# MLP in eight stages of d_ff, with w_down as a 2x2x2 Strassen scheme whose weight sums run on GpSimd

## The chip, the cores and the metric

The kernel runs on one core of one Trainium2 chip. The metric is device time in microseconds (us), from the first to the last instruction of the program with what the runtime lays around it; lower is better. A core has a matrix engine (PE, TensorE), three engines for element-wise work (DVE or VectorE, ACT or ScalarE, POOL or GpSimd) and a sync engine (SP) that issues the DMAs here. SBUF is the on-chip memory, PSUM the memory into which PE writes its products.

## The reference

One layer of a hybrid decoder on 256 tokens of width 2048, in float32. The change touches only the MLP behind the mixers (D_FF is 8192):

```python
    for l in range(DEPTH):
        x = x + hybrid_mixer(x, ln_mix_g[l], w_in[l], ...)
        hm = rmsnorm(x, ln_mlp_g[l]) @ w_up[l]
        x = x + jnp.square(jax.nn.relu(hm)) @ w_down[l]
    return rmsnorm(x, final_g)
```

`w_up` is 2048 x 8192, `w_down` 8192 x 2048. Each is 64 MB and is read once.

## The kernel before

**Precision.** Every float32 operand of a large product is split into two parts that PE takes in its faster float32 format: `hi` is the rounded value, `lo` what is left. A product of two split operands is made of three matmuls (hi hi, hi lo, lo hi). ACT writes `hi` (a cast), DVE then writes `lo = raw - hi`.

**Weight stream.** The weights arrive in pieces of 1 MB (128 partitions x 2048), in the order of use, through one queue of SP. A piece is split in two units of 128 x 1024 (`split_unit`, L131 for `hi` on ACT, L132 for `lo` on DVE). `advance(h)` is called ahead of each unit's matmuls; it issues loads up to 12 units and splits up to 4 units ahead. The buffers are 4 for `raw` and 5 each for `hi` and `lo`.

**The MLP.** d_ff is worked through in four quarters. In a quarter, 16 pieces of `w_up` come first: `mm_t` (L218, L219) multiplies a 128 x 128 tile of w_up with all 256 tokens; the moving operand holds both parts of the tokens side by side, so a `hi` weight runs 512 columns and a `lo` weight 256. DVE and ACT then add the halves, square what is above zero and split the result into `u` (L672 to L677). After this come 16 pieces of `w_down`, in four chunks of 512 output columns: `mm_n` (L237 to L239) takes, for each of 16 tiles of d_ff and each of the two token halves, three matmuls of 512 columns. A chunk is 96 matmuls and ends with an update of the residual `xr` on DVE (L691, PSUM and SBUF in). The last chunk is followed by the final norm and the output's DMAs.

**Order.** POOL runs in program order; on the other engines a scheduler places the instructions by priority and readiness, and the splits have a raised priority. Apart from the mixers and the final norm (L697, `xr` times the norm's gain) POOL has no work.

Of the kernel before, what the change touches and what calls it, by code (L numbers as in the profile page):

```python
# [14 lines left out]
P = 128  # L15
# [8 lines left out]
DFF = 8192  # L24
NQ = 4
# [4 lines left out]
DMA_AHEAD = 12  # L30
# [11 lines left out]
# columns of the packed per-partition vectors  # L42
# [10 lines left out]
# pieces of the packed rows  # L53
# [5 lines left out]
def trunk(ctx: ExitStack, tc: tile.TileContext, x, xt, w_t, w_n, w_o, w_u, w_d, gw, gm_w, cols, rows, out):  # L59
    nc = tc.nc  # L60
    const = ctx.enter_context(tc.tile_pool(name="const", bufs=1))
    big = ctx.enter_context(tc.tile_pool(name="big", bufs=1))
    wpool = ctx.enter_context(tc.tile_pool(name="wpool", bufs=W_BUFS))
    work = ctx.enter_context(tc.tile_pool(name="work", bufs=1))
    two = ctx.enter_context(tc.tile_pool(name="two", bufs=2))
    small = ctx.enter_context(tc.tile_pool(name="small", bufs=1))
    acc = ctx.enter_context(tc.tile_pool(name="acc", bufs=2, space=PSUM))
    misc = ctx.enter_context(tc.tile_pool(name="misc", bufs=4, space=PSUM))
# [18 lines left out]
    def load_piece():
# [3 lines left out]
        if j == 0:  # L91
            for i in range(4):
                if i < 2:
                    ks = slice(0, 1) if i == 0 else slice(1, 4)
                    nc.sync.dma_start(xs4[:, ks, :], xt3[:, ks, :])
                nc.sync.dma_start(raw[:, i * 512:(i + 1) * 512], pieces[j][:, i * 512:(i + 1) * 512])
        elif j < 4:
            for i in range(2):
                k = 4 * j + 2 * i
                nc.sync.dma_start(xs4[:, k:k + 2, :], xt3[:, k:k + 2, :])  # L100
                nc.sync.dma_start(raw[:, i * 1024:(i + 1) * 1024], pieces[j][:, i * 1024:(i + 1) * 1024])
        else:
            nc.sync.dma_start(raw, pieces[j])
# [10 lines left out]

    def split_unit():
        """w = hi + lo exactly, both in float32r's significand."""
        h = state["split"]
        state["split"] += 1
        parts = 1
        if h < 4 * UNITS:  # L120
            kn = 4 // UNITS
            for k in range(h * kn, (h + 1) * kn):
                x_prep(k)
            parts = 2 if h < P2 else 1
        raw = raws[h // UNITS][:, h % UNITS * UW:(h % UNITS + 1) * UW]
        hi = wpool.tile([P, UW], F32R, tag="hi", name=f"hi{h}")
        lo = wpool.tile([P, UW], F32R, tag="lo", name=f"lo{h}")
        n = UW // parts
        for i in range(parts):
            s = slice(i * n, (i + 1) * n)  # L130
            nc.scalar.copy(hi[:, s], raw[:, s])  # L131
            nc.vector.tensor_tensor(out=lo[:, s], in0=raw[:, s], in1=hi[:, s].bitcast(F32), op=ALU.subtract)  # L132
        his[h], los[h] = hi, lo
        if h % UNITS == UNITS - 1:
            raws.pop(h // UNITS)

    def advance(h):
# [36 lines left out]
    # constants that the mixers use  # L174
    cmask = const.tile([P, P], F32, name="cmask")
# [18 lines left out]
    def diag_broadcast(dst, col2, name):  # L194
        """dst[p, t] = col2[t % P, t // P] on every partition p."""
# [28 lines left out]
    def mm_n(pt, act, j, tail=0):  # L224
# [3 lines left out]
        n = 4 * UNITS  # L228
# [17 lines left out]
        if tail:  # L246
            advance(j * UNITS + n - 1)
# [14 lines left out]
    mm_n(pt, xg, 0)  # L262
# [524 lines left out]
```

## Time and profile before

| | |
|---|---|
| median of 3 runs | 1108.7 us (1108.28 to 1109.09) |
| span of the profiled execution | 1106.8 us; its whole time is not listed apart, the median of the runs is 1.9 us more than this span |
| PE busy | 1096.3 us, 99% |
| DVE busy | 693.6 us, 63% |
| ACT busy | 529.0 us, 48% |
| POOL busy | 56.6 us, 5% |
| granted PE clock | 0.998 of full speed |
| DMA | 211 MB, 190 GB/s of HBM over the span |

Busy time of PE is the sum of pipelined instructions, so its share only says that PE nearly always had something in flight. How long a stage takes is better read from the start times of its instructions, or from the windows of the stages. The times of DVE and POOL instructions in a timeline are from issue to completion: an instruction that is held up after its issue shows a longer duration, not idle time ahead of it.

### The profile page before, as it was taken

Reading aid. Unit: us, or ns where it says so; the run is one execution under the profiler, and the core shown is the slowest. Engines: PE = TensorE matmul, PEld = TensorE weight load, DVE = VectorE, ACT = ScalarE, POOL = GpSimd, SP = SyncE. Lnnn points to the kernel's source line nnn. Section 1 sums busy time; section 2 is a strip of 40 time slices with the busy share of each in tenths; the row PEclk is TensorE's granted clock in tenths of the full one; section 3 lists DMA queues with packets and bytes.
Section 4 is the critical chain, followed back from the end, with each engine's and each line's share of the span. In section 5 each row is a group of like instructions: output and inputs, shape, how many; then the busy total and the mean of one; then the engine's idle time right before and its main releaser. Section 6 shows DMA issues by size and latency. Waiting matters only on the chain.

```text
span 1106.8 us, 13675 instructions
## 1 busy us (share of the span) xinstructions
PE 1096.3 (99%) x5447; PEld 924.4 (84%) x5447; DVE 693.6 (63%) x841; ACT 529.0 (48%) x655; POOL 56.6 (5%) x70
## 2 busy tenths in 40 slices
PE   9999999999999999999999999999999999999997
PEld 7888888888888888888888888888888888888885
DVE  6799999565765566555456565455565545565553
ACT  7575754545554454443344443334444334444442
POOL 1002110040300000000000000000000000000111
PEclk9999999999999999999999999999999999999999
DMA  9645545455475555555555555555555555555541
GB/s 341 265 171 190 170 173 190 159 184 191 158 299 189 190 191 184 183 186 198 199 191 183 181 181 198 198 197 183 181 182 192 198 197 192 179 184 187 194 144 76
DMA packets 32175, 211.05 MB, mean 191 GB/s; under 512 B 3696, under 2 KB 4080, under 8 KB 7664
## 3 DMA queue, kind: packets, MB, share of 16 engines
q1 hardware_dynamic: 32112, 210.19, 53.9%
q8 instruction: 42, 0.69, 0.2%
q14 instruction: 21, 0.17, 0.0%
HBM read 208.08 MB, written 2.10 MB: 190 GB/s over the span
## 4 chain that ended last, share of the span: by engine, by line
PE 95%; issue 2%; DMA 1%; ACT 1%; POOL 1%; SPq 0%; DVE 0%; ACTq 0%; POOLq 0%
PE up L218 20%; PE up L219 10%; PE dn L239 10%; PE dn L237 10%; PE dn L238 10%; PE qk L218 5%; PE wo L237 3%; PE wo L239 3%; PE wo L238 3%; PE qk L219 3%; PE up L222 1%; PE o L237 1%; PE o L239 1%; PE o L238 1%; PE v L237 1%
## 5 line engine op out<-in xcount | busy, mean ns | idle before, releaser
L132 DVE TENSOR_TENSOR lo<-raw,hi 128x1024 fp32r<-128x1024 f32 (+1 forms) x388 | 477.7, 1233 | 365.8 <-ACT hi L131 364.9
L131 ACT CAST hi<-raw 128x1024 fp32r<-128x1024 f32 (+1 forms) x388 | 403.2, 1042 | 516.1 <-PE dn L239 188.7
L218 PE MATMUL up<-x,hi 128*128 128x512 f32 x960 | 341.9, 399 | 0.0
L219 PE MATMUL up<-x,lo 128*128 128x256 f32 x960 | 269.7, 281 | 0.0
L218 PEld LDWEIGHTS up<-x,hi 128*128 128x128 f32 x960 | 180.4, 188 | 41.6
L237 PE MATMUL dn<-hi,u 128*128 128x512 f32 x480 | 186.7, 389 | 0.0
L238 PE MATMUL dn<-lo,u 128*128 128x512 f32 x480 | 186.7, 389 | 0.0
L239 PE MATMUL dn<-hi,u 128*128 128x512 f32 x480 | 186.7, 389 | 0.0
L219 PEld LDWEIGHTS up<-x,lo 128*128 128x128 f32 x960 | 181.3, 189 | 3.1
L238 PEld LDWEIGHTS dn<-lo,u 128*128 128x128 f32 x480 | 90.1, 188 | 18.9
L239 PEld LDWEIGHTS dn<-hi,u 128*128 128x128 f32 x480 | 90.1, 188 | 18.8
L237 PEld LDWEIGHTS dn<-hi,u 128*128 128x128 f32 x480 | 90.1, 188 | 18.3
L218 PE MATMUL qk<-xg,hi 128*128 128x512 f32 x240 | 85.8, 400 | 0.0
L219 PE MATMUL qk<-xg,lo 128*128 128x256 f32 x240 | 67.4, 281 | 0.0
L310 DVE SCALAR_TENSOR_TENSOR cvo<-aT,colv,cvo 128x256 f32<-128x256 f32 x120 | 55.1, 511 | 0.0
L218 PEld LDWEIGHTS qk<-xg,hi 128*128 128x128 f32 x240 | 45.1, 188 | 10.5
L237 PE MATMUL wo<-hi,mix 128*128 128x512 f32 x128 | 50.4, 394 | 0.0
L238 PE MATMUL wo<-lo,mix 128*128 128x512 f32 x128 | 50.1, 391 | 0.0
L239 PE MATMUL wo<-hi,mix 128*128 128x512 f32 x128 | 49.9, 390 | 0.0
L697 POOL TENSOR_TENSOR xr<-xr,fgv 128x512 f32<-128x512 f32 x6 | 9.5, 1606 | 771.3 <-ACT jf L695 771.3
L219 PEld LDWEIGHTS qk<-xg,lo 128*128 128x128 f32 x240 | 45.3, 189 | 0.7
L239 PEld LDWEIGHTS wo<-hi,mix 128*128 128x128 f32 x128 | 24.0, 188 | 5.0
(232 smaller groups left out, 1076.0 us busy)
## 6 DMA issues: line engine op xcount, KB each, us to landing
raw<-in_w_u SPq DMA_DIRECT2D x64, 1024.0 KB, 4.7
raw<-in_w_d SPq DMA_DIRECT2D x64, 1024.0 KB, 4.7
raw<-in_w_n SPq DMA_DIRECT2D x28, 1024.0 KB, 4.7
raw<-in_w_t SPq DMA_DIRECT2D x16, 1024.0 KB, 4.8
raw<-in_w_o SPq DMA_DIRECT2D x16, 1024.0 KB, 4.8
raw<-in_w_n SPq DMA_DIRECT2D x6, 512.0 KB, 8.3
xr<-in_x SPq DMA_DIRECT2D x2, 1024.0 KB, 6.4
out<-xr SPq DMA_DIRECT2D x8, 256.0 KB, 2.6
```

The source lines that it names most:

```text
L131: nc.scalar.copy(hi[:, s], raw[:, s])
L132: nc.vector.tensor_tensor(out=lo[:, s], in0=raw[:, s], in1=hi[:, s].bitcast(F32), op=ALU.subtract)
L218: nc.tensor.matmul(pt[:, i, :], start=(k == 0), stop=False, **a)
L219: nc.tensor.matmul(pt[:, i, 0:T], start=False, stop=False, **b)
L222: nc.tensor.matmul(pt[:, i, :], start=False, stop=True, **a)
L237: nc.tensor.matmul(pt[t], lhsT=xh, rhs=hi[:, kk, :], start=(k == 0), stop=False)
L238: nc.tensor.matmul(pt[t], lhsT=xh, rhs=lo[:, kk, :], start=False, stop=False)
L239: nc.tensor.matmul(pt[t], lhsT=xl, rhs=hi[:, kk, :], start=False, stop=(k == NK - 1))
L310: nc.vector.scalar_tensor_tensor(out=o, in0=a, scalar=w, in1=o, op0=ALU.mult, op1=ALU.add)
L697: nc.gpsimd.tensor_tensor(out=xr[:, t, cs], in0=xr[:, t, cs], in1=fgv[:, cs], op=ALU.mult)
```

## The change

**Stages.** d_ff is cut into eight stages of 1024. Stage 0's eight w_up pieces run alone. Then, for each of seven stages, eight slots follow: a slot is one piece of w_down of this stage (`dn_piece`) and one piece of w_up of the next (`up_tile`). In the last stage there are four w_down slots alone, and its second half of the output columns is done the old way (`mm_n`, two chunks of 48 matmuls).

**Strassen.** A w_down slot covers two tiles of d_ff (256 rows) and 1024 output columns, that is, four weight blocks of 128 x 512, and the two token halves. The 8 block products become 7, so 21 matmuls instead of 24. PE's 1536 matmuls of 512 columns for w_down become 60 x 21 + 96 = 1356. The matmuls of w_up stay 64 tiles of 32.

**Weight sums.** For each of the 60 w_down slots POOL forms four sums of blocks in three instructions (`sum_piece`): one of 128 x 1024 (two sums that share a block, into `sa`), and two of 128 x 512 (into `sb`). There are two buffers for these, one for `sa` and one for `sb`. ACT and DVE then split 1536 + 1024 + 1024 columns per w_down piece (three blocks of `raw`, then `sa`, `sb`) where it was 2048.

**Activations.** After a w_up tile ACT copies one half, DVE adds the halves (L769, PSUM and SBUF in), takes the part above zero times the norm's factor `rb` (L770, both inputs in SBUF), and ACT squares it into `uf` (L771). For each pair of tiles POOL forms four sums in three instructions (L773, L775, L776), and ACT and DVE split seven blocks of 128 (`split_pair`, L791).

**Results.** Every four slots `dn_out` works the seven products into `xr`: a copy on ACT, seven additions on DVE (each with one input in PSUM, one in SBUF) and four of 128 x 512 on POOL (all in SBUF).

The core of the diff:

```diff
+    for st in range(NS - 1):
+        for sl in range(2 * NP):
+            jdn[st, sl] = len(pieces)
+            pieces.append((w_pair(st, sl), True))
+            jup[st + 1, sl] = len(pieces)
+            pieces.append((w_u[(st + 1) * 2 * NP + sl], False))
...
+    def sum_piece():
+
+        j = state["sum"]
+        state["sum"] += 1
+        if not pieces[j][1]:
+            return
+        raw = raws[j]
+        s13 = ph["mlp"].tile([P, 1024], F32, tag="sum", name=f"sa{j}", bufs=2)
+        s24 = ph["mlp"].tile([P, 1024], F32, tag="sum", name=f"sb{j}", bufs=2)
+        nc.gpsimd.tensor_tensor(out=s13.rearrange("p (a n) -> p a n", a=2),
+                                in0=raw[:, 512:1536].rearrange("p (a n) -> p a n", a=2),
+                                in1=raw[:, 0:512].rearrange("p (a n) -> p a n", a=1).broadcast_to([P, 2, 512]),
+                                op=ALU.add)
+        nc.gpsimd.tensor_tensor(out=s24[:, 0:512], in0=s13[:, 512:1024], in1=raw[:, 512:1024], op=ALU.add)
+        nc.gpsimd.tensor_tensor(out=s24[:, 512:1024], in0=s24[:, 0:512], in1=raw[:, 1536:2048], op=ALU.add)
+        sums[j] = (s13, s24)
...
+        if not pieces[j][1]:
+            src, n, tag, pool, bufs = raws[j][:, k * UW:(k + 1) * UW], UW, "", wpool, None
+        elif k == 0:
+            src, n, tag, pool, bufs = raws[j][:, 512:2048], 1536, "3", ph["mlp"], 2
+        else:
+            src, n, tag, pool, bufs = sums[j][k - 1], 1024, "", wpool, None
...
+        while state["sum"] < len(pieces) and state["sum"] <= j + SUM_AHEAD:
+            with tc.high_priority(HP):
+                sum_piece()
...
+        nc.vector.tensor_tensor(out=q, in0=pt[:, 0:T], in1=sb, op=ALU.add)
+        nc.vector.scalar_tensor_tensor(out=q, in0=q, scalar=0.0, in1=rb, op0=ALU.max, op1=ALU.mult)
+        nc.scalar.activation(u[:, 0:8:7, :] if i == 0 else u[:, 1:3, :], q.rearrange("p (t n) -> p t n", t=2), AF.Square)
+        if i == 1:
+            nc.gpsimd.tensor_tensor(out=u[:, S3:S1 + 1, :], in0=u[:, A21:A21 + 1, :].broadcast_to([P, 2, P]),
+                                    in1=u[:, A11:A22 + 1:2, :], op=ALU.subtract)
+            nc.gpsimd.tensor_tensor(out=u[:, S2, :], in0=u[:, A11, :], in1=u[:, S1, :], op=ALU.subtract)
+            nc.gpsimd.tensor_tensor(out=u[:, S4, :], in0=u[:, A12, :], in1=u[:, S2, :], op=ALU.subtract)
...
+        for k, prods in enumerate((((A11, 1), (S4, 0), (A12, 2)), ((S1, 1), (S3, 0)), ((S2, 0), (A22, 1)))):
+            advance(h0 + k)
+            hi, lo = his.pop(h0 + k), los.pop(h0 + k)
+            for a, b in prods:
...
+                nc.tensor.matmul(acc7[a], lhsT=ah, rhs=hi[:, cs], start=(g == 0), stop=False)
+                nc.tensor.matmul(acc7[a], lhsT=ah, rhs=lo[:, cs], start=False, stop=False)
+                nc.tensor.matmul(acc7[a], lhsT=al, rhs=hi[:, cs], start=False, stop=(g == NP - 1))
...
+        p1, v, w = (mlp.tile([P, 512], F32, tag=n, name=f"{n}{st}_{pn}") for n in ("p1", "v", "w"))
+        nc.scalar.copy(p1, acc7[A11])
+        dve(x12, x12, acc7[S4], ALU.add)
+        dve(x11, x11, acc7[A12], ALU.add)
+        dve(x12, x12, acc7[S1], ALU.add)
+        dve(x22, x22, acc7[S1], ALU.add)
+        dve(v, p1, acc7[S2], ALU.subtract)
+        dve(w, v, acc7[S3], ALU.subtract)
+        dve(x21, x21, acc7[A22], ALU.add)
+        pool(x11, x11, p1, ALU.add)
+        pool(x12, x12, v, ALU.subtract)
+        pool(x21, x21, w, ALU.add)
+        pool(x22, x22, w, ALU.subtract)
...
+    for st in range(NS - 1):
+        for sl in range(2 * NP):
+            pn, g = divmod(sl, NP)
+            if g == 0:
+                acc7 = {}
+            dn_piece(st, sl, acc7)
+            if pn == 1 and g < NP - 1:
+                split_pair(st + 1, g)
+            if g == NP - 1:
+                dn_out(st, pn, acc7)
+            up_tile(st + 1, sl)
+        split_pair(st + 1, NP - 1)
```

**POOL's order.** This is POOL's queue of the kernel before from the end of the mixers to the program's end (`lnc` and `og` belong to the mixers):

```order
L192 TENSOR_TENSOR lnc<-lnr,nhalf 128x2
L605 TENSOR_TENSOR og<-og,numx 128x512 x2
L697 TENSOR_TENSOR xr<-xr,fgv 128x512 x6
L192 TENSOR_TENSOR rf<-rf,nhalf 128x1 x2
```

The change puts 336 instructions of the MLP ahead of the last two of these lines: 180 for sums of weights, 96 for sums of activations, 60 for `xr`. This is POOL's queue of the change for two slots of the first mixed stage and the end of its first four slots:

```order
L159 TENSOR_TENSOR sa_3943<-raw_3749 128x1024
L163 TENSOR_TENSOR sb_3944<-sa_3943,raw_3749 128x512
L164 TENSOR_TENSOR sb_3944<-sb_3944,raw_3749 128x512
L159 TENSOR_TENSOR sa_4034<-raw_3847 128x1024
L163 TENSOR_TENSOR sb_4035<-sa_4034,raw_3847 128x512
L164 TENSOR_TENSOR sb_4035<-sb_4035,raw_3847 128x512
L823 TENSOR_TENSOR xr<-xr,p_0_4072 128x512
L823 TENSOR_TENSOR xr<-xr,v_0_4073 128x512
L823 TENSOR_TENSOR xr<-xr,w_0_4074 128x512 x2
L773 TENSOR_TENSOR uf_1_4024<-uf_1_4024 128x256
L775 TENSOR_TENSOR uf_1_4024<-uf_1_4024 128x128
L776 TENSOR_TENSOR uf_1_4024<-uf_1_4024 128x128
```

What moved: weight sums, the updates of `xr` and the sums of activations stand in one queue, each behind the one ahead of it.

**DVE's order.** This is DVE's queue of the kernel before for one pair of w_up tiles (all `raw` are w_up pieces):

```order
L132 TENSOR_TENSOR lo_4777<-raw_4590,hi_4776 128x1024
L674 TENSOR_TENSOR u_t_4768<-up_4681,u_sb_4766 128x512
L675 SCALAR_TENSOR_TENSOR u_t_4768<-u_t_4768 128x512
L132 TENSOR_TENSOR lo_4797<-raw_4590,hi_4796 128x1024
L677 TENSOR_TENSOR u_4588<-u_t_4768,u_4588 128x2x256
L132 TENSOR_TENSOR lo_4819<-raw_4632,hi_4818 128x1024
L132 TENSOR_TENSOR lo_4839<-raw_4632,hi_4838 128x1024
```

And this is DVE's queue of the change for one slot of the first mixed stage (`raw_4031` is the w_down piece of the slot after next, `raw_3982` a w_up piece):

```order
L769 TENSOR_TENSOR uq_3_4132<-up_3_4087,usb_3_4130 128x256
L770 SCALAR_TENSOR_TENSOR uq_3_4132<-uq_3_4132,rb 128x256
L190 TENSOR_TENSOR lo_4262<-raw_4031,hi_4261 128x1536
L791 TENSOR_TENSOR us_0_4187<-uf_0_3840,us_0_4187 128x7x128
L190 TENSOR_TENSOR lo_4176<-sa_4142,hi_4175 128x1024
L190 TENSOR_TENSOR lo_4194<-sb_4143,hi_4193 128x1024
L190 TENSOR_TENSOR lo_4214<-raw_3982,hi_4213 128x1024
L190 TENSOR_TENSOR lo_4249<-raw_3982,hi_4248 128x1024
L190 TENSOR_TENSOR lo_4272<-sa_4243,hi_4271 128x1024
```

What moved: the splits of w_down's sums (`sa`, `sb`) stand between those of `raw`, and wait on POOL's sums and ACT's casts of them; the splits of w_up stand behind them in the same queue.

## Rows read from the trace of the kernel before

**Rows 1.** The page, parts 1 and 4: busy time by engine, and the chain

```profile
PE 1096.3 (99%) x5447; PEld 924.4 (84%) x5447; DVE 693.6 (63%) x841; ACT 529.0 (48%) x655; POOL 56.6 (5%) x70
...
PE 95%; issue 2%; DMA 1%; ACT 1%; POOL 1%; SPq 0%; DVE 0%; ACTq 0%; POOLq 0%
```

**Rows 2.** Waits in total, DVE's largest (us, times, longest)

```profile
DVE lo L132 <- ACT hi L131: 364.9, 285, 2.4
```

**Rows 3.** Windows: head, one w_up and one w_down stage, last stage (columns as header)

```profile
core 0: us, PE busy (x) PEld busy (x) DVE busy (x) ACT busy (x) POOL busy (x), PEclk, DMA share, GB/s
0.00:387.60 387.60, 385.29 (x1856) 321.55 (x1857) 293.89 (x442) 220.69 (x311) 46.00 (x62) 1.00 0.57 205
...
566.20:656.90 90.70, 90.70 (x515) 78.66 (x514) 53.76 (x55) 40.96 (x47) 0.00 (x0) 1.00 0.54 186
656.90:743.90 87.00, 87.00 (x386) 72.09 (x385) 45.28 (x42) 34.74 (x35) 0.00 (x0) 1.00 0.56 194
```

**Rows 4.** Timeline, DVE from 71 us (start, duration, instruction)

```profile
71.26 1.22 DVE L132 TENSOR_TENSOR lo<-raw,hi 128x1024 fp32r<-128x1024 f32 x1
72.40 0.68 DVE L410 TENSOR_TENSOR qk_t<-qk,qk_sb 128x512 f32<-128x512 f32 x1
73.00 1.35 DVE L310 SCALAR_TENSOR_TENSOR cvo<-aT,colv,cvo 128x256 f32<-128x256 f32 x2
...
75.96 2.06 DVE L421 SCALAR_TENSOR_TENSOR qk_c<-qk_z,colv,qk_c 128x256 f32<-128x256 f32 x5
```

**Rows 5.** Timeline, POOL: two instructions with no DVE instruction at their start

```profile
241.03 0.73 POOL L551 TENSOR_TENSOR csum<-cvo 128x256 f32<-128x256 f32 x1
...
275.58 1.30 POOL L605 TENSOR_TENSOR og<-og,numx 128x512 f32<-128x512 f32 x1 [31.25 <-ACT og L603]
```

**Rows 6.** Timeline, DVE and POOL from 232 us

```profile
232.81 1.22 DVE L132 TENSOR_TENSOR lo<-raw,hi 128x1024 fp32r<-128x1024 f32 x1
232.97 2.21 POOL L508 TENSOR_TENSOR gv<-gv,gng 128x512 f32<-128x512 f32 x1 [0.66 <-DVE gv L506]
...
235.26 1.34 POOL L509 TENSOR_TENSOR gv<-gv,gng 128x512 f32<-128x512 f32 x1
235.39 4.52 DVE L132 TENSOR_TENSOR lo<-raw,hi 128x1024 fp32r<-128x1024 f32 x2
236.56 2.27 POOL L508 TENSOR_TENSOR gv<-gv,gng 128x512 f32<-128x512 f32 x1
...
238.91 2.16 POOL L509 TENSOR_TENSOR gv<-gv,gng 128x512 f32<-128x512 f32 x1
```

**Rows 7.** Timeline, DVE and POOL from 1034 us

```profile
1034.71 1.22 DVE L132 TENSOR_TENSOR lo<-raw,hi 128x1024 fp32r<-128x1024 f32 x1
1035.19 3.14 POOL L697 TENSOR_TENSOR xr<-xr,fgv 128x512 f32<-128x512 f32 x2 [734.18 <-ACT jf L695]
1037.24 2.16 DVE L132 TENSOR_TENSOR lo<-raw,hi 128x1024 fp32r<-128x1024 f32 x1 [1.32 <-ACT hi L131]
```

**Rows 8.** Timeline, DVE and POOL from 284 us

```profile
284.39 1.29 POOL L568 TENSOR_TENSOR sq<-sq 128x512 f32<-128x512 f32 x1 [5.85 <-ACT sq L567]
285.28 1.48 DVE L132 TENSOR_TENSOR lo<-raw,hi 128x1024 fp32r<-128x1024 f32 x1 [0.94 <-ACT hi L131]
285.76 1.60 POOL L569 TENSOR_TENSOR sq<-sq 128x256 f32<-128x256 f32 x1
286.69 0.68 DVE L520 TENSOR_TENSOR mix<-hbT,mix 128x512 fp32r<-128x512 f32 x1
```

**Rows 9.** Timeline, PE's last matmul

```profile
1098.23 0.39 PE L239 MATMUL dl<-hi,u 128*128 128x512 f32 x1
```

**Rows 10.** Windows behind it (columns as in rows 3)

```profile
1100.00:1102.00 2.00, 0.00 (x0) 0.00 (x0) 1.07 (x3) 1.09 (x4) 0.55 (x1) 1.00 0.00 0
1102.00:1104.00 2.00, 0.00 (x0) 0.00 (x0) 0.29 (x1) 0.47 (x1) 0.00 (x0) 0.75 0.75 286
1104.00:1107.00 3.00, 0.00 (x0) 0.00 (x0) 0.00 (x0) 0.00 (x0) 0.00 (x0) 0.50 0.41 159
```

More of the change, by code (lines that the diff above doesn't have):

```diff
@@ L653, in trunk @@
     r2 = const.tile([P, 2], F32, name="r2")
+    rb = const.tile([P, T], F32, name="rb")
     nc.vector.tensor_reduce(out=r2, in_=st2, op=ALU.add, axis=mybir.AxisListType.X)
     nc.vector.tensor_scalar(out=r2, in0=r2, scalar1=1.0 / D, scalar2=EPS, op0=ALU.mult, op1=ALU.add)
[L656 to L662 removed]
@@ new lines, in trunk, with bank @@
+    rsqrt_cols(r2, r2, 2)
+    mixers.close()
+    mlp = ph["mlp"] = ctx.enter_context(tc.tile_pool(name="mlp", bufs=1, reuse_waits="tile"))
+    banks = ctx.enter_context(tc.tile_pool(name="banks", bufs=8, space=PSUM, reuse_waits="tile"))
+    def bank(name):
+        return banks.tile([P, 512], F32, tag="bank", name=name)
+    st3 = const.tile([P, 2, 4], F32, name="st3")
+    ssf = const.tile([P, 2], F32, name="ssf")
+    rf = const.tile([P, 2], F32, name="rf")
+    A11, A12, A22, S3, S1, S2, S4, A21 = range(8)
@@ new lines, in trunk, with up_units @@
+    uf, us = {}, {}
+    def up_units(pt, j, k):
+        kn = NK // UNITS
+        h = first[j] + k
+        hi = his.pop(h).rearrange("p (k n) -> p k n", k=kn)
+        lo = los.pop(h).rearrange("p (k n) -> p k n", k=kn)
+        for kk in range(kn):
+            kt = k * kn + kk
+            a = dict(lhsT=hi[:, kk, :], rhs=x2[:, kt, :, :])
+            b = dict(lhsT=lo[:, kk, :], rhs=x2[:, kt, 0, :])
+            if kt < NK - 1:
+                nc.tensor.matmul(pt, start=(kt == 0), stop=False, **a)
+                nc.tensor.matmul(pt[:, 0:T], start=False, stop=False, **b)
+            else:
+                nc.tensor.matmul(pt[:, 0:T], start=False, stop=False, **b)
+                nc.tensor.matmul(pt, start=False, stop=True, **a)
@@ new lines, in dn_out, with dve, pool @@
+    def dn_out(st, pn, acc7):
+        c1, c2 = (slice((2 * pn + i) * 512, (2 * pn + i + 1) * 512) for i in range(2))
+        x11, x12, x21, x22 = xr[:, 0, c1], xr[:, 0, c2], xr[:, 1, c1], xr[:, 1, c2]
+        def dve(out, a, b, op):
+            nc.vector.tensor_tensor(out=out, in0=a, in1=b, op=op)
+        def pool(out, a, b, op):
+            nc.gpsimd.tensor_tensor(out=out, in0=a, in1=b, op=op)
+        p1, v, w = (mlp.tile([P, 512], F32, tag=n, name=f"{n}{st}_{pn}") for n in ("p1", "v", "w"))
[11 more added lines that the diff above has]
+        pool(x22, x22, w, ALU.subtract)
@@ new lines, in trunk @@
+    for k in range(UNITS):
+        for sl in range(2):
+            j = jup[0, sl]
+            if k == 0:
+                us["pt", sl] = bank(f"up0_{sl}")
+            advance(first[j] + k if k == sl else first[jup[0, 0]] + 2 * k + sl)
+            up_units(us["pt", sl], j, k)
+    rps = bank("rps")
+    for t in range(2):
+        dg = mlp.tile([P, P], F32, tag="usb", name=f"r_dg{t}")
+        nc.vector.tensor_scalar(out=dg, in0=ident, scalar1=r2[:, t:t + 1], scalar2=None, op0=ALU.mult)
+        nc.tensor.matmul(rps[:, t * P:(t + 1) * P], lhsT=ones, rhs=dg, start=True, stop=True)
@@ new lines, in trunk @@
+    nc.vector.tensor_copy(rb, rps[:, 0:T])
+    for sl in range(2):
+        up_out(us.pop(("pt", sl)), 0, sl)
+    split_pair(0, 0)
+    for sl in range(2, 2 * NP):
+        up_tile(0, sl)
+        if sl % 2:
+            split_pair(0, sl // 2)
+    for st in range(NS - 1):
+        for sl in range(2 * NP):
+            pn, g = divmod(sl, NP)
+            if g == 0:
+                acc7 = {}
[6 more added lines that the diff above has]
+        split_pair(st + 1, NP - 1)
@@ new lines, in trunk, with act_last @@
+    st = NS - 1
+    fgv = keep.tile([P, D], F32, tag="A", name="fgv")
+    nc.sync.dma_start(fgv, rows[0:1, R_FG:R_FG + D].broadcast_to([P, D]))
+    acc7 = {}
+    for sl in range(NP):
+        dn_piece(st, sl, acc7)
+    dn_out(st, 0, acc7)
+    def act_last(k, t):
+        g, i = divmod(k, 2)
+        if i == 0 and t == 1:
+            return us["a21"][:, g, 0, :], us["a21"][:, g, 1, :]
+        a = A11 if i == 0 else A12 if t == 0 else A22
+        return us[st, g][:, a, 0, :], us[st, g][:, a, 1, :]
```

277 lines of the change are left out of this document (158 added, 119 removed).

## The prediction

> **What bounds the kernel now.** I read the page first, then the waits, then the windows of the MLP's stages. The page shows PE busy for 99% of the span and 95% of the chain on PE [rows 1]. In the waits DVE's largest is for ACT's cast, in 285 short waits of at most 2.4 us; casts and splits run ahead and wait for a free buffer, so neither engine sets the pace [rows 2]. The windows give PE's rate: the MLP starts at 387.6, a stage of 16 w_up tiles takes 90.7 us, one of 384 w_down matmuls 87.0 us, both at the full clock (1.00), with DVE busy for only 54 and 45 us and POOL idle [rows 3]. So a w_up tile costs PE 5.67 us and a w_down matmul 0.2266 us. A piece of each now takes PE 5.67 + 24 x 0.2266 = 11.11 us.
>
> **What is removed.** 1536 - 1356 = 180 matmuls, 180 x 0.2266 = 40.8 us. A slot then costs PE 5.67 + 21 x 0.2266 = 10.43 us. If PE stayed the bound, the span would go from 1106.8 to 1066. So everything hangs on whether the other engines serve a slot in 10.43 us.
>
> **What is added, by engine, for one slot.** First the prices.
>
> DVE: a 128x1024 split is followed by the next instruction after 1.14 us (71.26 to 72.40), a 128x512 one after 0.60 [rows 4]; that is 1.055 ns a column, so 1536 columns cost 1.68, 896 cost 1.00, 256 cost 0.33. A two-input instruction of 256 columns out of SBUF costs 2.06 / 5 = 0.41 [rows 4].
>
> POOL: alone, 0.73 us for 256 columns and 1.30 for 512 [rows 5], 2.2 ns a column.
>
> Now the row that decides. From 235.26 on POOL runs three 512-column products while DVE has two splits. The splits take 4.52 us together, where 2.28 would do, and POOL's second and third take 2.27 and 2.16 where one alone takes 1.30 [rows 6, 5]. All five end at 238.91 + 2.16 = 241.07, 5.81 us after the first started. Two splits at 1.14 leave 3.53 for three products, 1.18 each: the engines took turns, one whole instruction at a time. The other places agree: the product issued at 232.97, just behind a split that runs to 234.03, ends at 235.18, 1.15 us behind that split [rows 6]; and the split issued at 1037.24 takes 2.16, ending at 1039.40, 1.07 us behind POOL's second product, which ends at 1038.33 [rows 7]. All of these have two inputs in SBUF on both engines. One case differs: at 286.69 DVE starts a split with one input in PSUM while POOL's product runs until 287.36, and needs its usual 0.68 [rows 8]. So I count DVE instructions with two SBUF inputs and all of POOL's sums as serial, and DVE's with one input in PSUM as free to run beside POOL.
>
> Prices for POOL by turns: 512 columns 1.18; by 2.2 ns a column 1024 cost 2.32, 256 cost 0.61, 128 cost 0.33. The 1024-column sum reads one block twice, which no row shows; I bound it by 1024 columns at the slope alone, 2.25, and by two products of 512 with nothing saved, 2.60; either end moves the sum by under 16 us over 56 slots.
>
> POOL per slot: weight sums 2.32 + 2 x 1.18 = 4.68. Activation sums, one set in two slots: (0.61 + 2 x 0.33) / 2 = 0.64. Updates of `xr`, four in four slots: 1.18. Together 6.50 us.
>
> DVE with two SBUF inputs per slot: splits 1.68 + 4 x 1.14 = 6.24, half a split of 896 columns 0.50, L770 0.41. Together 7.15 us.
>
> DVE with one input in PSUM per slot: L769 0.33, seven additions in four slots 7 x 0.60 / 4 = 1.05. Together 1.38 us.
>
> So what must go in turn is 6.50 + 7.15 = **13.65 us a slot**, against PE's 10.43. If no PSUM instruction found POOL at work beside it, a slot would be 13.65 + 1.38 = 15.03. These are the two bounds. One rule is weighed against the single row behind that 1.38. The Trainium skill ("SBUF — State Buffer", section "Who interferes with whom") says that a DVE instruction with at most one SBUF input and outside the two-port modes does not contend with GpSimd; by it the sum may come down to 13.65, and without it, it would be 15.03. Rows 8 agree with it, in one place.
>
> Which end? I follow the two queues through four slots. DVE's order has the split of the sums behind L769 and L770, the w_up splits behind these; POOL has `xr`'s updates and the activation sums ahead of the next weight sums, and only one `sa` and one `sb`. POOL can sum the next `sa` when DVE has split the last. While POOL sums, DVE waits for its turn or for a cast; while DVE adds PSUM results in `dn_out`, POOL mostly has nothing ready, since its next work needs what these additions write (`x11`, `v`, `w`). So most of the 1.38 isn't covered: about 1.1 of it. ACT's cast of `sa` (1.05) falls beside POOL's `sb` sums. I take **14.8 us a slot**. Chains between the engines (L769, L770, ACT's square, three sums, `sa`, cast, split) could add up to 1 us more; this gives the range an upper end of about 16.1.
>
> What was hidden: ACT has 3584 + 2048 columns to cast and some small work, some 7.5 us a slot, below 14.8, at nothing. DMA brings the same bytes in a longer time, at nothing. The mixers are untouched.
>
> **The sum.** The MLP starts at 387.6. Eight w_up tiles: 8 x 5.67 = 45.4, to 433.0. 56 slots at 14.8: 828.8, to 1261.8. Four w_down slots alone: 4.68 + 1.68 + 2 x 1.14 = 8.64 us in turn, the first half prepared: 3.5 x 8.64 = 30, to 1292. The rest of the last slot's matmuls 1.5, the 96 old-style matmuls 21.8, to 1315.5. From the last matmul at 1098.2 to the end of the span it was 8.6 [rows 9], and stays: 1324 of span. The median of the runs is 1.9 above the span of the profiled execution: **1326 us**, 20% slower. In general the time is 497 + 56 x slot.
>
> **The rivals.**
>
> *No turns (faster).* If POOL's sums held DVE up little, DVE would need 7.15 + 1.38 = 8.53 us a slot, below PE's 10.43, and PE would give 1066 + 1.9 = 1068. The time equals that of now at a slot of 10.92 us, so at most 10.92 - 8.53 = 2.4 of POOL's 6.50 us may hold DVE up. For it speaks that profile times of POOL are rough; against it that DVE's own durations grow by the same turns in rows 6, 7 and 8. 4% for faster, 1% for no change. Between it and the next (slots of 10.95 to 13.65, 1110 to 1260): 6%, if POOL's price or the share of turns is overestimated.
>
> *Full cover.* All PSUM additions find POOL at work: slots of 13.65 to 14.3, 1261 to 1298. For it: POOL has 6.5 us of work a slot to lay them beside. Against it: POOL's next work depends on them. 20%.
>
> *PE's clock falls.* PE would be idle for 14.8 - 10.43 = 4.4 us a slot. The rows behind its last matmul, which ends at 1098.6, show a granted clock of 1.00 up to 1102, 0.75 in the next window and 0.50, the lower level of 1.2 GHz, from 1104 on, with PE idle all the while [rows 9, 10]. In short waits, unit by unit, it may stay up; gathered ahead of `sa`, once in two slots, it may fall as there. It decides only if more than (14.8 - 10.43) / 10.43 = 42% of the matmuls run at half rate; at 70% a slot is 10.43 x 1.7 = 17.7 us and the time 1490. The Trainium skill ("TensorE: Matmul & The Clock Gate", section "HAM oscillation — how this bites in real kernels") describes a kernel whose every tile starts cold behind a wait; no wait inside this trace is long enough to show it. 12%.
>
> **How the numbers follow.** My case is a slot of 14.3 to 15.6 us, 1298 to 1371: 52%. Longer chains without a clock loss, 15.6 to 16.5, up to 1420: 5%. The range 1255 to 1400 takes in my case, full cover, most of the longer chains and the milder half of the clock case, about 8 in 10. 0.2% is 2.2 us, about what can be told from no change here. Faster 4%, same 1%, slower 95%.
>
> **What would show it.** Right: DVE splits that last 2.2 to 3.6 us beside POOL's sums where they now last 1.22; POOL busy for more than half of the MLP by the profile, its 512-column sums often over 2 us; PE at some 70% in the mixed stages, waiting for `lo` of the sums and of w_up; a stage of eight slots of about 118 us. Wrong: splits of 1.22 us beside POOL's sums and PE without waits (no turns), or a granted clock well under 1.00 in the mixed stages and matmul spacings of 0.45 us (the clock).

## The result, and the profile after

The changed kernel takes **1363.8 us** (median of 4 runs, 1363.34 to 1366.06) against 1108.5 for the kernel before on the same chip: a ratio of 1.231, 95% interval 1.2294 to 1.2327. 1326 was predicted, with a range of 1255 to 1400. The profiled execution took 1366.06 us with a span of 1364.4; as in [rows 1] the page's part 1 gives each engine's busy time, part 2's PEclk the granted clock in 40 slices, part 4 the shares of the chain:

```profile
PE 1162.5 (85%) x5271; PEld 936.5 (69%) x5271; DVE 997.5 (73%) x1048; ACT 652.4 (48%) x830; POOL 616.0 (45%) x407
...
PEclk9999999999999788888979888888979888888979
```

PE's busy time rose from 1096.3 to 1162.5 us though it has 180 matmuls fewer; its share fell from 99% to 85% of a longer span, and its clock is below full in most slices from the first mixed stage on. On the chain of work that ended last PE now holds 36%, POOL 26% and DVE 23%, where PE held 95%; DVE's splits (L190) are the largest share of a line with 16%. The windows of the first w_up tiles, of one mixed stage of eight slots, and of the end (columns as in [rows 3]):

```profile
389.00:434.30 45.30, 45.30 (x262) 39.48 (x261) 29.60 (x39) 23.91 (x36) 11.07 (x12) 1.00 0.44 155
679.60:802.30 122.70, 97.44 (x426) 76.88 (x425) 90.50 (x75) 53.51 (x63) 74.23 (x44) 0.86 0.38 137
1292.90:1332.40 39.50, 27.61 (x88) 19.43 (x87) 26.89 (x24) 14.45 (x17) 27.37 (x16) 0.78 0.39 143
1332.40:1354.50 22.10, 22.09 (x98) 17.96 (x96) 14.77 (x22) 10.19 (x20) 14.53 (x11) 1.00 0.00 1
1354.50:1364.40 9.90, 0.00 (x0) 0.00 (x0) 3.10 (x6) 3.39 (x6) 1.04 (x2) 0.75 0.55 212
```

There are three stretches to see. The first tiles end at 434.3 (433.0 predicted). The mixed part runs from there to 1292.9: 858.6 us for 56 slots, **15.33 us a slot** (14.8 predicted). In its stage POOL is busy for 60% of the time and PE for 79%, part of that at the lower clock: eight slots hold 8 x 10.43 = 83.4 us of PE's work at full clock, 68% of the 122.7. The last stage takes 61.6 us (30 + 1.5 + 21.8 = 53.3 predicted), what follows it 9.9 (8.6).

Where DVE and POOL both have two inputs in SBUF at the same time, the timelines of DVE and of POOL from 849 us show the turns (DVE's rows first, then POOL's; start, duration, instruction, idle time before and who ended it):

```profile
849.65 1.34 DVE L190 TENSOR_TENSOR lo<-sa,hi 128x1024 fp32r<-128x1024 f32 x1 [3.37 <-ACT hi L189]
853.25 2.34 DVE L190 TENSOR_TENSOR lo<-sb,hi 128x1024 fp32r<-128x1024 f32 x1 [2.26 <-ACT hi L189]
855.51 3.44 DVE L190 TENSOR_TENSOR lo<-raw,hi 128x1024 fp32r<-128x1024 f32 x2
858.88 2.31 DVE L190 TENSOR_TENSOR lo<-sa,hi 128x1024 fp32r<-128x1024 f32 x1
861.12 0.41 DVE L769 TENSOR_TENSOR uq<-up,usb 128x256 f32<-128x256 f32 x1
861.45 0.67 DVE L820 TENSOR_TENSOR xr<-xr,dn 128x512 f32<-128x512 f32 x1
849.98 2.15 POOL L164 TENSOR_TENSOR sb<-sb,raw 128x512 f32<-128x512 f32 x1
852.09 2.41 POOL L159 TENSOR_TENSOR sa<-raw 128x1024 f32<-128x1024 f32 x1
855.73 2.15 POOL L163 TENSOR_TENSOR sb<-sa,raw 128x512 f32<-128x512 f32 x1 [1.23 <-DVE lo L190]
857.95 2.16 POOL L164 TENSOR_TENSOR sb<-sb,raw 128x512 f32<-128x512 f32 x1
```

The split that starts at 853.25 finds POOL's sum at work until 854.50; it ends 1.09 us after that, as if it had begun there. POOL's next sum, issued at 855.73, takes 2.15 where one alone takes 1.30 [rows 5]. Over the whole run the groups of instructions show the same (mean ns of one behind the busy time):

```profile
L190 DVE TENSOR_TENSOR lo<-raw,hi 128x1024 fp32r<-128x1024 f32 x260 | 360.3, 1398 | 89.4 <-ACT hi L189 89.2
L159 POOL TENSOR_TENSOR sa<-raw 128x1024 f32<-128x1024 f32 x60 | 165.7, 2762 | 0.0
L164 POOL TENSOR_TENSOR sb<-sb,raw 128x512 f32<-128x512 f32 x60 | 127.9, 2132 | 4.7
L190 DVE TENSOR_TENSOR lo<-sb,hi 128x1024 fp32r<-128x1024 f32 x60 | 104.1, 1736 | 68.9 <-ACT hi L189 68.9
L190 DVE TENSOR_TENSOR lo<-sa,hi 128x1024 fp32r<-128x1024 f32 x60 | 103.2, 1721 | 91.3 <-ACT hi L189 91.3
L820 DVE TENSOR_TENSOR xr<-xr,dn 128x512 f32<-128x512 f32 x75 | 49.3, 673 | 0.0
```

The splits of `sa` and `sb` mean 1.72 and 1.74 us instead of 1.22, the second `sb` sum 2.13; the additions with an input in PSUM keep their 0.67, as in [rows 8].

**A wait that was not predicted.** From the waits (us in total, times, longest):

```profile
POOL uf L773 <- ACT uf L771: 199.3, 19, 14.9
...
PE dn L811 <- DVE xr L820: 67.0, 28, 3.1
PE up L754 <- DVE uq L769: 52.7, 15, 4.5
PE dn L812 <- DVE lo L190: 49.9, 46, 4.3
```

I had named the last as what PE would wait for; two others come before it. The first, 67.0 us, is that of a new group of block products for the additions of `dn_out`, which read the old products out of the same banks. The second comes from the same shortage. Seven of the eight PSUM banks hold the block products, so a w_up tile can only use the one that is left, and this is free when DVE has done L769 on the tile before. L769 is short, but in DVE's order it stands behind splits that wait for POOL. The timeline around 891 us, DVE's rows and then PE's, and the windows there show what comes of it:

```profile
891.38 2.28 DVE L190 TENSOR_TENSOR lo<-sa,hi 128x1024 fp32r<-128x1024 f32 x1
893.58 0.41 DVE L769 TENSOR_TENSOR uq<-up,usb 128x256 f32<-128x256 f32 x1
894.05 0.79 PE L754 MATMUL up<-x,hi 128*128 128x512 f32 x1 [3.65 <-DVE uq L769]
894.64 0.41 PE L755 MATMUL up<-x,lo 128*128 128x256 f32 x1
894.85 0.63 PE L754 MATMUL up<-x,hi 128*128 128x512 f32 x1
895.28 0.41 PE L755 MATMUL up<-x,lo 128*128 128x256 f32 x1
...
900.46 0.40 PE L754 MATMUL up<-x,hi 128*128 128x512 f32 x1
900.69 0.28 PE L755 MATMUL up<-x,lo 128*128 128x256 f32 x1
...
901.85 0.40 PE L811 MATMUL dn<-hi,us 128*128 128x512 f32 x1
```
```profile
890.00:894.00 4.00, 0.40 (x1) 0.00 (x0) 3.99 (x3) 2.34 (x2) 2.50 (x2) 0.50 0.22 29
894.00:898.00 4.00, 3.95 (x12) 3.37 (x13) 3.97 (x4) 2.19 (x3) 0.00 (x0) 0.50 0.87 361
898.00:902.00 4.00, 4.00 (x23) 3.51 (x22) 2.62 (x3) 1.05 (x1) 0.00 (x0) 0.91 0.33 134
902.00:906.00 4.00, 4.00 (x20) 3.26 (x19) 1.21 (x3) 2.28 (x3) 1.93 (x4) 1.00 0.72 262
```

PE stands still for 3.65 us, its granted clock is 0.50 (1.2 GHz), and a 512-column matmul of the tile holds it for 0.43 us (894.85 to 895.28) where 0.23 do at the upper level (900.46 to 900.69). The tile lasts 7.80 us (894.05 to 901.85) and not 5.67. Meanwhile POOL has nothing to do (0.00 in both windows from 894 to 902), for its next sums, those of `uf`, need that tile. This comes once in four slots: 14 tiles of the mixed part wait so and then last 7.49 to 8.33 us.

### The profile page after: what moved, and what is told of

Same layout as the page of the kernel before. It is cut to its first block, busy times and chain, and to the rows that moved or that the text cites. A ratio compares the mean times of both kernels' runs of the same rounds, so it can differ in the third digit from the quotient of the medians.

```text
span 1364.4 us, 14305 instructions
## 1 busy us (share of the span) xinstructions
PE 1162.5 (85%) x5271; PEld 936.5 (69%) x5271; DVE 997.5 (73%) x1048; ACT 652.4 (48%) x830; POOL 616.0 (45%) x407
## 4 chain that ended last, share of the span: by engine, by line
PE 36%; POOL 26%; DVE 23%; issue 11%; ACT 4%; DMA 0%; POOLq 0%; SPq 0%; DVEq 0%; ACTq 0%
DVE lo L190 16%; POOL sa L159 7%; PE up L754 6%; POOL sb L164 5%; PE qk L281 4%; POOL xr L823 4%; POOL sb L163 3%; POOL uf L773 3%; PE up L755 3%; ACT hi L189 3%; DVE xr L820 2%; PE wo L301 2%; PE wo L303 2%; PE wo L302 2%; PE qk L282 2%
## 5 line engine op out<-in xcount | busy, mean ns | idle before, releaser
L190 DVE TENSOR_TENSOR lo<-raw,hi 128x1024 fp32r<-128x1024 f32 (+2 forms) x328 | 486.8, 1495 | 126.6 <-ACT hi L189 126.4
L189 ACT CAST hi<-raw 128x1024 fp32r<-128x1024 f32 (+2 forms) x328 | 360.7, 1114 | 235.3 <-PE dn L813 44.7
L754 PE MATMUL up<-x,hi 128*128 128x512 f32 x960 | 370.5, 424 | 57.1 <-DVE uq L769 52.7
L811 PE MATMUL dn<-hi,us 128*128 128x512 f32 x420 | 187.0, 445 | 80.7 <-DVE xr L820 67.0
L812 PE MATMUL dn<-lo,us 128*128 128x512 f32 x420 | 188.7, 449 | 49.9 <-DVE lo L190 49.9
L813 PE MATMUL dn<-hi,us 128*128 128x512 f32 x420 | 182.6, 435 | 0.0
L190 DVE TENSOR_TENSOR lo<-sa,hi 128x1024 fp32r<-128x1024 f32 x60 | 103.2, 1721 | 91.3 <-ACT hi L189 91.3
L811 PEld LDWEIGHTS dn<-hi,us 128*128 128x128 f32 x420 | 88.6, 211 | 118.4 <-DVE xr L820 80.5
L159 POOL TENSOR_TENSOR sa<-raw 128x1024 f32<-128x1024 f32 x60 | 165.7, 2762 | 0.0
L190 DVE TENSOR_TENSOR lo<-sb,hi 128x1024 fp32r<-128x1024 f32 x60 | 104.1, 1736 | 68.9 <-ACT hi L189 68.9
L773 POOL TENSOR_TENSOR uf<-uf 128x256 f32<-128x256 f32 x32 | 44.8, 1399 | 199.3 <-ACT uf L771 199.3
L164 POOL TENSOR_TENSOR sb<-sb,raw 128x512 f32<-128x512 f32 x60 | 127.9, 2132 | 4.7
L163 POOL TENSOR_TENSOR sb<-sa,raw 128x512 f32<-128x512 f32 x60 | 107.0, 1783 | 39.7 <-DVE lo L190 37.2
L813 PEld LDWEIGHTS dn<-hi,us 128*128 128x128 f32 x420 | 90.5, 215 | 19.3
L771 ACT ACTIVATE uf<-uq 128x256 f32<-128x256 f32 x64 | 26.6, 417 | 117.9 <-DVE uq L770 117.9
```

The lines of the kernel that those rows point to most:

```text
L159: nc.gpsimd.tensor_tensor(out=s13.rearrange("p (a n) -> p a n", a=2), in0=raw[:, 512:1536].rearrange("p (a n) -> p a n", a=2), in1=raw[:, ...
L163: nc.gpsimd.tensor_tensor(out=s24[:, 0:512], in0=s13[:, 512:1024], in1=raw[:, 512:1024], op=ALU.add)
L164: nc.gpsimd.tensor_tensor(out=s24[:, 512:1024], in0=s24[:, 0:512], in1=raw[:, 1536:2048], op=ALU.add)
L189: nc.scalar.copy(hi[:, s], src[:, s])
L190: nc.vector.tensor_tensor(out=lo[:, s], in0=src[:, s], in1=hi[:, s].bitcast(F32), op=ALU.subtract)
L754: nc.tensor.matmul(pt, start=(kt == 0), stop=False, **a)
```

## The experiments

**Is it POOL's reading that holds DVE up?** The theory of turns says that POOL's sums cost DVE their duration because both read two SBUF inputs. The rivals: POOL's sums are only late, or PE's clock makes the time. The kernels of this part, and the two with sums on DVE behind it, ran once each; the differences that count are far above the 0.2% by which the runs of the change spread. The first attempt left the sums in place and took away who reads them:

```diff
-            src, n, tag, pool, bufs = sums[j][k - 1], 1024, "", wpool, None
+            src, n, tag, pool, bufs = raws[j][:, (k - 1) * 1024:k * 1024], 1024, "", wpool, None
```

> POOL forms the same weight sums as the change, but nobody reads them: the splits of those units take two plain halves of the raw piece instead, so the output is not that of the reference. No split waits for a sum any more; POOL's work and its inputs are as before. Theory of turns (DVE instructions with two SBUF inputs and POOL's sums go one after the other): the turn work of a slot is still 13.65 us, so a slot stays between 13.6 and 15.0 us and the time between 1260 and 1340 us; splits beside POOL's sums still last 2.0 us and more. Theory of waits (POOL is merely too late with its sums, or the queues wait for each other): with those waits gone a slot falls to PE's 10.4 to 11 us, 1080 to 1115 us.

1377.2 us, outside both expectations: the waits have a new entry, 319.1 us in all in which ACT's cast waits for the load of `raw`: POOL's sums, still late, hold the buffers. So it separates nothing. The same with a constant tile as the source of the split (`src = ph["fix"]`, a part of `x2`):

> As the run with sums that nobody reads, but the splits of those two units take 1024 columns of a tile that is there from the start, so that a raw buffer comes free as early as in the change (in the first version of it casts waited 319 us for w_down's loads). The output is not that of the reference. Theory of turns: 13.65 to 15.0 us a slot, 1260 to 1345 us. Theory of late sums: 10.4 to 11.5 us a slot, 1080 to 1145 us.

1369.0 us, outside both expectations, with 266.4 us of the same wait; it did not separate them either. Then POOL's sums were replaced by memsets of about their length, on which the splits still wait:

```diff
...
-        nc.gpsimd.tensor_tensor(out=s24[:, 512:1024], in0=s24[:, 0:512], in1=raw[:, 1536:2048], op=ALU.add)
+        for w in (1024, 1024, 512):
+            nc.gpsimd.memset(s13[:, 0:w], 0.0)
+        for o in (0, 512):
+            for w in (512, 512, 256):
+                nc.gpsimd.memset(s24[:, o:o + w], 0.0)
```

> The reverse: in place of each weight sum POOL writes constants for about as long (memsets of 2560, 1280 and 1280 columns, which read nothing), and the casts and splits wait for them as they waited for the sums; the weight sums are left out, so the output is not that of the reference. Theory of turns, if it is POOL's reading of SBUF that makes DVE wait: the turn work of a slot falls to 7.15 + 1.82 = 8.97 us, a slot comes near PE's 10.4 to 12 us and the time to 1080 to 1170 us, and splits beside a memset last 1.22 us. Theory of waits for late sums: POOL is as late as before, 1310 to 1370 us. If memsets too take turns with DVE: 1260 to 1340 us and long splits beside them.

1203.2 us: 160 less than the change, but above the expectation of turns, with the cast of `sa` still waiting 106.1 us in all for POOL. The splits beside the memsets are short, as that expectation said (1.22 and 1.24 us in the mean, where the change has 1.72 and 1.74):

```profile
L189 DVE TENSOR_TENSOR lo<-sb,hi 128x1024 fp32r<-128x1024 f32 x60 | 74.5, 1241 | 22.7 <-ACT hi L188 21.5
L189 DVE TENSOR_TENSOR lo<-sa,hi 128x1024 fp32r<-128x1024 f32 x60 | 73.3, 1221 | 94.6 <-ACT hi L188 94.6
```

Memsets also free the raw buffers early, so I built a pair that has this in common. In both the splits take a constant tile and nothing waits for POOL's weight work. In one POOL adds halves of the constant tile, in the other it writes memsets:

```diff
-                                in0=raw[:, 512:1536].rearrange("p (a n) -> p a n", a=2),
+                                in0=ph["fix"][:, 512:1536].rearrange("p (a n) -> p a n", a=2),
...
-            src, n, tag, pool, bufs = sums[j][k - 1], 1024, "", wpool, None
+            src, n, tag, pool, bufs = ph["fix"][:, 0:1024], 1024, "", wpool, None
```

> One of a pair. POOL forms sums of the same sizes, but of a tile that is there from the start, and nobody reads them; the splits of those two units take 1024 columns of the same tile. So no split, load or buffer hangs on a weight sum any more, while POOL still reads SBUF as much as in the change. The weight sums are left out, so the output is not that of the reference. Theory of turns: 13.6 to 15.3 us a slot, 1260 to 1360 us. Theory of late sums: 10.4 to 11.5 us a slot, 1080 to 1145 us.

> The other of the pair: as the one before, but POOL writes constants for about the same time instead of forming sums, so that it reads no SBUF for them; splits and casts are as there. The output is not that of the reference. Theory of turns: only 1.82 us of POOL's work a slot still takes turns with DVE, 8.97 us of turn work, below PE's 10.43: 1085 to 1160 us, at least 150 us below its pair. Theory that POOL's busy time or its queue, and not its reading, is what costs: within 30 us of its pair.

With POOL's reads **1281.7 us**, with its memsets **1090.4 us**. The window of 680 to 800 us, first of the reads, then of the memsets:

```profile
680.00:800.00 120.00, 101.00 (x459) 83.15 (x458) 114.45 (x78) 56.22 (x66) 90.66 (x47) 0.87 0.44 149
```
```profile
680.00:800.00 120.00, 116.30 (x581) 97.41 (x580) 106.27 (x104) 72.54 (x86) 94.93 (x131) 0.99 0.57 192
```

POOL is as busy in the one as in the other (90.66 and 94.93 us), yet PE gets 459 matmuls done with the reads and 581 with the memsets, at a clock of 0.87 and 0.99. Single rows, first of the kernel with reads (DVE, then POOL), then of that with memsets:

```profile
704.40 3.43 DVE L190 TENSOR_TENSOR lo<-x,hi 128x1024 fp32r<-128x1024 f32 x1
707.76 2.31 DVE L190 TENSOR_TENSOR lo<-raw,hi 128x1024 fp32r<-128x1024 f32 x1
709.99 1.27 DVE L821 TENSOR_TENSOR xr<-xr,dn 128x512 f32<-128x512 f32 x2
702.83 3.92 POOL L159 TENSOR_TENSOR sa<-x 128x1024 f32<-128x1024 f32 x1
706.83 2.16 POOL L163 TENSOR_TENSOR sb<-sa,x 128x512 f32<-128x512 f32 x1
709.07 2.13 POOL L164 TENSOR_TENSOR sb<-sb,x 128x512 f32<-128x512 f32 x1
```
```profile
708.81 1.22 DVE L189 TENSOR_TENSOR lo<-x,hi 128x1024 fp32r<-128x1024 f32 x1
709.95 1.22 DVE L189 TENSOR_TENSOR lo<-raw,hi 128x1024 fp32r<-128x1024 f32 x1
708.48 2.54 POOL L160 MEMSET sa<- 128x1024 f32 x3
```

The split issued at 704.40 ends at 707.83, 1.08 us behind POOL's sum (706.75). The two additions at 709.99 take 0.64 each while POOL's sum runs to 711.20. Beside memsets the splits take 1.22. So the two engines take turns where both read, and POOL's writing alone does not hold DVE up. The Trainium skill says the same ("SBUF — State Buffer", section "Who interferes with whom"): a DVE instruction with two SBUF inputs contends with a GpSimd instruction that reads SBUF, not with one that only writes it. The rows agree, 3.43 against 1.22 us.

The four kernels make a table. Reading, with all that follows from it (PE's lower clock among it), costs 161 us where the splits wait for POOL's result and 191 where they don't; that wait costs 82 us with turns and 113 without. In the upper row more than the wait differs: in the change POOL's sums also hold the `raw` buffers until they are done, in the kernel of 1281.7 us they don't. The memsets of a slot take 5.2 us and the sums, with their waiting for turns, 7.1 (310.5 and 428.0 us over 60 slots). So these are no exact shares.

| | splits wait for POOL | splits take a constant tile |
|---|---|---|
| POOL adds (reads SBUF) | 1363.8 (the change) | 1281.7 |
| POOL writes memsets | 1203.2 | 1090.4 |

**What if DVE does the sums itself?** `nc.gpsimd` becomes `nc.vector` in the three weight sums, and then in all sums of the MLP:

> The three weight sums of a slot are moved from POOL to DVE, all else is as in the change and the result is complete. DVE then has 8.53 + 2.4 = 10.9 us of work a slot, and POOL's remaining 1.82 us of sums take turns with it. Theory of turns: a slot of 11.5 to 12.9 us, 1140 to 1220 us, faster than the change though the busiest engine gets more work. Theory that it is DVE's own load or the chain from sums to casts to splits: as slow as the change or slower, 1340 to 1480 us.

1202.5 us, as expected.

> All of POOL's sums of the MLP (weights, activations, updates of xr) are on DVE; the result is complete. DVE then has 8.53 + 2.4 for weight sums, 0.5 for activation sums and 0.6 for xr, 12.0 us a slot, and nothing takes turns. Theory of turns: 12.0 us a slot, 1165 to 1185 us, faster than the run with the weight sums alone on DVE (1202) though DVE gets 1.1 us more work a slot. Theory that DVE's load or the chains set the time: 1202 us and more, up to 1265.

1206.2 us, 21 above the upper end of the expectation of turns and inside that for DVE's own load (1202 to 1265), and no better than the one before: what the last turns had cost came back as work of DVE. In the window of 680 to 800 us DVE is busy for 112.56 of 120 us and POOL for none: (1206.2 - 497) / 56 = 12.7 us a slot, bound by DVE, 0.7 us a slot above my sum for it. So with Strassen on every slot none of the three divisions of the sums comes near 1108.5; without turns, DVE has too little room for them.

**What does the bank loop cost?** ACT copies all 512 columns of a w_up tile out of PSUM, so that its bank waits for ACT and not for DVE:

```diff
-        sb = mlp.tile([P, T], F32, tag="usb", name=f"usb{st}_{sl}")
-        nc.scalar.copy(sb, pt[:, T:2 * T])
-        q = mlp.tile([P, T], F32, tag="uq", name=f"uq{st}_{sl}", bufs=2)
-        nc.vector.tensor_tensor(out=q, in0=pt[:, 0:T], in1=sb, op=ALU.add)
+        sb = mlp.tile([P, 2 * T], F32, tag="usb", name=f"usb{st}_{sl}")
+        nc.scalar.copy(sb, pt)
+        q = sb[:, 0:T]
+        nc.vector.tensor_tensor(out=q, in0=sb[:, 0:T], in1=sb[:, T:2 * T], op=ALU.add)
```

> After a w_up tile ACT copies both halves out of PSUM (512 columns for 256), and DVE adds them from SBUF. The bank is then free after ACT's copy; in the change the next w_up tile waited for DVE's addition L769, 15 waits and 52.7 us in total. If this closed loop (w_up tile, L769 behind DVE's splits, next w_up tile) is what makes a slot 15.3 us where turns alone give 14.8: 1330 to 1345 us. If the turns fill that time anyway: 1355 to 1375 us, since L769 now has two SBUF inputs and takes a turn too.

1342.4 us, ratio 1.2116 (1.208 to 1.2151): 21 us less than the change, as expected.

**And the clock?** More matmuls were put in (they repeat a product, so the output is not exact): first five behind each of the three units of a slot, then eight in one slot of four, in the pause ahead of the w_up tile:

> Five more matmuls of 512 columns behind each of the three units of a w_down slot (they add one product five times too often, so the output is not that of the reference): PE gets 3.4 us more work a slot, 13.8 us in all, still under the 15.3 us that a slot takes, and has shorter pauses. Theory that the fallen clock costs time (w_up tiles at half rate where the chain passes through them): the granted clock rises from 0.906 to 0.96 or more and the time falls to 1325 to 1350 us. Theory that turns set the time whatever PE does: the clock rises and the time stays within 1355 to 1375. If PE's work is itself on the path in most slots: 1380 us and more.

1380.4 us, ratio 1.2457 (1.2435 to 1.248): the mean granted clock rose from 0.906 to 0.972 and the time by 16 us, to the foot of what was expected if PE's work is itself on the path (1380 and more). The fillers' own time and the clock are mixed here, so it decides nothing.

```diff
+                for _ in range(8 if k == 2 and g == 1 and (a, b) == prods[-1] else 0):
+                    nc.tensor.matmul(acc7[a], lhsT=al, rhs=hi[:, cs], start=False, stop=False)
```

> The change with eight more matmuls of 512 columns in one slot of four, behind the last unit of the second w_down slot of each group, where PE then waits for the bank of the next w_up tile and runs that tile at half clock (they add a product too often, so the output is not that of the reference). They fit into that pause. Theory that the fallen clock costs time there (a w_up tile of 8.4 us on the chain instead of 5.7, once in four slots, 14 times): the tile is back near 5.7 us and the time falls to 1325 to 1345 us. Theory that the turns fill that time anyway: within 1358 to 1370 us. If the fillers don't fit the pause: above 1370 us.

1343.8 us, ratio 1.2128 (1.2105 to 1.215): 20 us less than the change though PE does more. Of the 14 tiles that lasted 7.49 us and more in the change, 11 now last 5.65 to 5.77; at some 2.1 us each that is 23 us. So the fallen clock costs some 20 us there. What it costs in all was not measured: PE is busy for 682.7 us in the mixed part of the change, 98.6 more than the 56 x 10.43 = 584.1 it would need at full clock, and how much of that stands on the path is not shown.

**A version that fits.** The bound on DVE leaves room for half: Strassen for the first 1024 columns of each stage (32 slots), 24 plain matmuls in each of the others, all sums on DVE:

```diff
-            dn_piece(st, sl, acc7)
...
+            if pn == 0:
+                dn_piece(st, sl, acc7)
+            else:
+                dn_plain(st, sl, pts)
```

> A version that may beat both: Strassen for the first 1024 output columns of each stage alone (32 slots of 21 matmuls), the other 1024 columns with 24 matmuls a piece and no sums, and all sums on DVE. The result is complete. PE saves 96 matmuls, 21.8 us; a stage is 86.2 us of PE's work, and DVE has 74 us in it. Theory of turns (with no turns and DVE below PE, PE is the bound again): 1087 to 1100 us. If the order of the queues alone costs what the change lost: 1130 us and more.

1102.1 us (1100.79 to 1104.98, 5 runs), ratio 0.995 (0.9936 to 0.9963): half a per cent faster than before, 2 us above the upper end of its expectation. Its last stage has no w_up to lay the sums beside; with plain matmuls there:

> The version with Strassen in half of the columns and all sums on DVE (1102 us), with the last stage done without Strassen at all, since no w_up tiles stand between its slots and PE waited there (the stretch behind the last w_up tile took 54.9 us for some 50 of PE's work). The result is complete. PE gets 12 matmuls more, 2.7 us; the waits of about 5 us should go: 1096 to 1101 us. If the time there is not due to Strassen's sums and their splits: 1104 to 1106 us.

**1099.6 us**, ratio 0.9923 (0.991 to 0.9937). A mixed stage and the end of it:

```profile
434.60:522.30 87.70, 85.96 (x435) 72.43 (x435) 75.86 (x96) 48.69 (x58) 0.00 (x0) 1.00 0.54 192
1046.60:1098.00 51.40, 42.65 (x187) 34.67 (x186) 27.54 (x36) 21.67 (x35) 9.54 (x8) 0.95 0.32 121
```

PE is busy for 85.96 of 87.70 us at the full clock and DVE for 75.86: PE is the bound again, and eight slots take 87.7 us where eight of the old kind took 8 x 11.11 = 88.9.

## Why the prediction was right

**What bounds the kernel, and what is removed.** PE's 10.43 us a slot held: with no weight sums to take turns with or to wait for (1090.4 us) a slot takes, by the formula of the prediction, (1090.4 - 497) / 56 = 10.6 us. Of the saving of 40.8 us that kernel shows 18 (1108.2 before it), 22 short of the 1068 that I gave; no kernel that forms all the sums comes near it.

**The turns.** Right, and shown by the pair: 191 us from POOL's reads and what follows from them. With turns and no wait for the sums a slot is (1281.7 - 497) / 56 = 14.0 us, between my bounds of 13.65 and 15.03. That an input in PSUM frees DVE also held (0.67 in the mean over 75).

**14.8 us a slot.** This is the term that was mis-sized: 15.33 measured, inside my case of 14.3 to 15.6; 0.53 x 56 = 30 of the 40 us by which the span of 1324 was low. I had 1.1 us for PSUM additions not covered, and nothing for the chains between the engines, which stood in the range alone ("up to 1 us more"). The pair of 1363.8 and 1281.7 says that waiting for the sums costs 82 / 56 = 1.5 us a slot, and 14.0 says that the additions, where POOL has something ready, cost 0.4 at most. If that holds for the change as well, the first number was too high and the second too low, they cancelled in part, and it is so far luck that 14.8 came near; in the change itself the two aren't separated. Of the 30 us by which the slots were too long, letting ACT empty the bank takes away 21, and filling the pause ahead of one tile in four 20. The tile at half clock stands behind the wait for the bank, so these may overlap, and both edits together weren't tried. They are not shares of the 82: with no wait for the sums PE still waits for the bank, longer than in the change (52.7), at a mean granted clock of 0.927 (row of the kernel of 1281.7 us):

```profile
PE up L755 <- DVE uq L770: 64.9, 16, 6.3
```

What the 82 us are made of (an only `sa`, an only `sb`, `raw` held until POOL has summed it) is argued from the waits, not shown; nor was the wait for `xr`, the longest of PE's, tested.

**The last stage.** 39.5 us for the four slots and the matmuls behind them, where 31.5 were predicted. I took POOL and DVE in turn with half the first slot prepared; the granted clock of 0.78 and PE busy for 27.61 of 39.50 say that nothing covers the chain sums, cast, split there. The tail took 9.9 and not 8.6.

**At nothing.** ACT (53.51 of 122.70 us busy) and the loads (137 GB/s, 38% of the DMA engines) stayed off the path, as costed.

**The rivals.** No turns is refuted by 3.43 against 1.22 us. Full cover, 13.65 to 14.3, is the place where the kernel without waits stands, but not the change. The clock did fall, 0.86 in the mixed stage, which I had listed as a sign against my case; what it costs in the tiles behind the bank is near 20 us, and the 98.6 us that PE was busy longer are 17% of its work at full clock, not the 42% from which on that rival would have set the time. My condition was too coarse: a low clock during a wait costs nothing, and what counts is which matmuls behind the wait run low before it returns. The Trainium skill ("TensorE: Matmul & The Clock Gate", section "HAM oscillation — how this bites in real kernels") describes tiles that start cold behind a wait; rows at 894.05 agree, with a wait of 3.65 us and a clock of 0.50.

**What would show it.** Splits of 2.3 us, POOL's second `sb` sum at 2.13, POOL at 60% of a stage were seen; PE was busy for 79% and not 70, its work at full clock would be 68%. Two signs against me were seen as well, a clock of 0.86 and spacings of 0.43 us, the second in the tile at 894. PE's waits were not those I named: for `xr` and for the bank first, for `lo` third. A stage of eight slots took 122.7 and not 118.

## What to carry to other kernels

Before moving work to an idle POOL, add its SBUF-reading time to DVE's time in instructions with two SBUF inputs: the sum is one queue, and here it was 13.65 us a slot against PE's 10.43. When a scheme needs more accumulators, count what is left of PSUM and who frees it: one spare bank ties PE to the slowest queue ahead of the instruction that frees it. If an idea saves on the bound and overloads another engine, do it on the share of the work that the other engine can carry: with the sums on DVE, Strassen in 28 of the 60 slots gave 0.8% where in all of them it cost 9% (1206.2 us); with the sums on POOL it cost 23%.

## What the runs showed of the hardware that was not expected

POOL's memsets leave DVE alone. Over all 120 splits of the constant tile the mean is 1.51 us in the kernel with memsets, whose activation sums and updates of `xr` on POOL still read, and 2.06 in its pair; with POOL as busy in both, that is 191 us of the run. In the turns the waiting time is counted as busy on both engines: with reads DVE stands at 114.45 of 120 us while it does less than with memsets at 106.27, so a busy share of these two engines, read alone, would have named DVE alone, and not the two in turn. A filler of eight matmuls in the right pause made the kernel 20 us faster; five behind each of three units made it 16 us slower.
